# The opening of a decoder layer in the order of its loads: chunks of four token tiles in one PSUM bank, norms of four tiles together

## The chip, the cores and the metric

The kernel runs on one core of one Trainium2 chip. TensorE (PE) multiplies matrices into PSUM, ScalarE (ACT) and VectorE (DVE) do elementwise work, GpSimd (POOL) a little of the rest, and SyncE (SP) issues most DMAs. The metric is the time of one execution on the device in microseconds; the time shown for a kernel is the median of its runs. A separate, profiled execution leaves a trace, whose first and last instruction bound its span.

## The reference

A hybrid decoder layer for 1024 tokens of width 1024 (one sequence): a gated feed-forward half step, a mixing step (sliding-window attention beside a state-space model), and another feed-forward half step. Each has a norm ahead, with shift, scale and gate columns made from a conditioning vector. Only the beginning matters here:

```python
c_act = jax.nn.silu(c)
mod = c_act @ w_ada[l] + b_ada[l]
(sh1, sc1, ga1, sh2, sc2, ga2, sh3, sc3, ga3) = jnp.split(mod, N_MOD, axis=-1)

h = modulate(rms_norm(x, g_pre_ff1[l]), sh1, sc1)     # h * (1 + scale) + shift
f = swiglu(h, w1_gate[l], w1_up[l], w1_down[l])       # D_FF = 2816
x = x + 0.5 * ga1[:, None, :] * rms_norm(f, g_post_ff1[l])
```

All is float32.

## The kernel before, in words

**Layout.** The 1024 tokens are eight token tiles of 128 tokens by 1024 features (`xs`). The feed-forward needs features on partitions, so each tile is turned: eight blocks ("feature chunks" k = 0 to 7) of 128 x 128. The turned activations are eight arrays `hf[k]` (tags `q0` to `q7`) of 128 features by 1024 tokens. The gate and up weights are stored by units u of two blocks f; units 0 and 1 are computed directly, and units 2 to 21 by seven products of a fast 2x2 scheme each (order 1, 5, 6, 2, 7, 3, 4), with sums of quarters of the activations (`s12`, `s34`).

**Precision.** Every float32 operand is split in a high and a low part: ScalarE casts the high part (`act.copy` in `split`, L69) and VectorE subtracts (L70). `mm3` (L74 to L76) then issues three matmuls of 128x128 by 128x512 per pair.

**Norm and turning.** `norm_diag` (L1353 to L1358) squares a tile on ScalarE with an accumulated sum (L156), makes the reciprocal root with one ScalarE root and five tiny VectorE operations (L141 to L145, L151), and writes a 128x128 diagonal of it. Turning a tile is a product of its 128x128 blocks with that diagonal (L207), so that it is normed on the way; a product in float32 leaves two PE records. Four blocks of one tile go into one PSUM bank and are evicted one by one, 128x128 each, by ScalarE (L218, or L222, which modulates at once) or VectorE (L220).

**Modulation.** `ada_in(k)` makes shift and scale of chunk k: two weighted row sums of a 128x1024 block of `w_ada` (`ada_block`, L166) and one tiny operation (L190). `modulate` (L1367) applies them to 512 tokens of a chunk on VectorE, and `g1.block` splits the result. For r = 1 and the chunks 0 to 3 it is applied in the eviction (L222).

**Passes.** `g1.first(r, c)` multiplies half r of the tokens (512) and half c of the features (4 chunks) with units 0 and 1: 4 chunks x 2 units x 2 blocks x 3 = 48 matmuls, into banks `b0` to `b3` for r = 0 and `b4` to `b7` for r = 1. The order is (0,0), (1,0), (0,1), and in `second_half` (1,1), after which silu, product and the sums of `s12` and `s34` follow and the seven-product units begin.

**Order.** In the opening the program's order is a wish: a scheduler places each engine's instructions by a timeline of its own. `pinned` (L80) is the other way: the instructions that a function issues keep their written order on each engine. Before the change it is used from the seven-product units on, not in the opening. Loads go through SP's queue in the written order: the conditioning row, four token tiles, ada blocks of chunks 0 to 2, weights of units 0 and 1 (c = 0), ada of chunk 3, four token tiles, ada of 4 to 6, weights (c = 1), ada of 7.

Of the kernel before, what the change touches and what calls it, by code (L numbers as in the profile page):

```python
# [11 lines left out]
F32R = mybir.dt.float32r  # L12
I32 = mybir.dt.int32
AF = mybir.ActivationFunctionType
# [3 lines left out]
P = 128  # L18
D = 1024
# [11 lines left out]
def tile_layer(ctx: ExitStack, tc: tile.TileContext, a: dict, out: bass.AP, stage: str = "all"):  # L31
# [33 lines left out]
    def names(c, *idx):  # L65
        return tuple(f"{c}{i}" for i in idx)

    def split(hi, lo, src, eng=dve):
        act.copy(hi, src)  # L69
        eng.tensor_tensor(lo, src, hi.bitcast(F32), op=SUB)  # L70

    def mm3(psum, wh, wl, xh, xl, first, last, goes_on=False):

        pe.matmul(psum, wh, xh, start=first, stop=False, skip_group_check=goes_on)  # L74
        pe.matmul(psum, wh, xl, start=False, stop=False, skip_group_check=goes_on)  # L75
        pe.matmul(psum, wl, xh, start=False, stop=last, skip_group_check=goes_on)  # L76
# [3 lines left out]
    def pinned(f, *args, hold=True):  # L80


        traced = nc.cur_bb.bb.instructions
        n = len(traced)
        r = f(*args)
        for i in list(traced[n:]):
            prev = last_of.get(i.engine)
            if prev is not None:
                tc.add_manual_dep(
                    i, prev.name, mybir.DependencyInfo(mybir.DependencyClass.NoSync, mybir.DependencyReason.DATA),  # L90
                    reason="pinned",
                )
            if hold:
                last_of[i.engine] = i
        return r
# [52 lines left out]
    def rstd_of(ss, n, count):  # L148

        v = small(n, "rsv")  # L150
        dve.tensor_scalar(v, ss, 1.0 / count, EPS, op0=MUL, op1=ADD)  # L151
        return rsqrt(v, n)

    def row_rstd(src, junk):
        ss = small(1, "ss")
        act.activation(junk, src, AF.Square, accum_out=ss)  # L156
        return rstd_of(ss, 1, D)
# [15 lines left out]
    def mod(v):  # L173
        return modc[:, 8 * v : 8 * v + 8]
# [35 lines left out]
    def to_hf(t, xs, hf, *ns, scale=None):  # L210

        for b, n in enumerate(ns):
            pt = turned(xs, b, scale)
            for kk in range(4):
                k = 4 * b + kk
                dst = hf[k][:, t * P : (t + 1) * P]
                if n is None and b == 0:
                    act.copy(dst, pt[:, kk, :])  # L218
                elif n is None:
                    dve.tensor_copy(dst, pt[:, kk, :])  # L220
                elif b == 0:
                    act.activation(  # L222
                        dst, pt[:, kk, :], AF.Identity, scale=gsc[:, n, k : k + 1], bias=mod(3 * n)[:, k : k + 1]
                    )
# [67 lines left out]
    class Weights:  # L292
# [66 lines left out]
    class GateUp:  # L359
# [34 lines left out]
                self.put("s4", k, self.q(0, 1, k))  # L394


        def first(self, r, c, between=None):
            for k in range(4):
                x = self.A[f"a{r + 1}{c + 1}"][k]
                for u in range(2):  # L400
                    for f in range(2):
                        if c == 0 and k == 0:
                            self.pb[r, u, f] = bank(f"b{4 * r + 2 * u + f}")
                        w = self.wt.ops[u, f, c][:, :, k * P : (k + 1) * P]
                        mm3(self.pb[r, u, f], w[:, 0], w[:, 1], x[:, 0], x[:, 1], c == 0 and k == 0, c == 1 and k == 3)
                if between:
                    between(k)

# [678 lines left out]
    def prep_phases():  # L1087
# [258 lines left out]
    ada_rot = Rot(*names("a", 8, 9, 10, 11, 12, 13, 14, 15, 20, 21, 22, 23, 12, 13, 14, 15))  # L1346
# [12 lines left out]

    def ada_in(k, ws):  # L1360
        for j, w in zip((8 + k, k), ws):
            ada_block(j, w)
        scale_cols(0, 1, slice(k, k + 1))

    def modulate(r, k):
        x = g1.q(r, k // 4, k % 4)
        dve.tensor_scalar(x, x, gsc[:, 0, k : k + 1], mod(0)[:, k : k + 1], op0=MUL, op1=ADD)  # L1367

    def loads(c):

        xs = [load_in_order(f"a{4 * c + t}", x_d[0][4 * c + t]) for t in range(4)]
        ada = []
        for k in range(4 * c, 4 * c + 4):
            if k % 4 == 3:
                for u in range(2):
                    w1.load(u, c)
            ada.append([load_in_order(ada_rot(), a["w_ada"][j]) for j in (8 + k, k)])
        return xs, ada

    xs, ada = loads(0)  # L1380
    for t in range(4):
        with tc.high_priority():
            to_hf(t, xs[t], hf, None, None, scale=norm_diag(t, 0))
    for k in range(4):
        ada_in(k, ada[k])
        modulate(0, k)
        g1.block(0, 0, k)
    w1.first(0)
    g1.first(0, 0)
    xs, ada = loads(1)  # L1390
    for t in range(4):
        to_hf(4 + t, xs[t], hf, 0, None, scale=norm_diag(t, 1))
    for k in range(4):
        g1.block(1, 0, k)
    g1.first(1, 0)
    for k in range(4, 8):
        ada_in(k, ada[k - 4])
        for r in range(2):
            modulate(r, k)
            g1.block(r, 1, k - 4)  # L1400
    w1.first(1)
    g1.first(0, 1)
    sp.dma_start(sink, a["sinks"].partition_broadcast(P))

    def second_half(g):
# [207 lines left out]
```

## Time and profile before

| what | before |
|---|---|
| median of 3 runs | 1717.06 us (1717.0 to 1725.35) |
| the profiled execution's own time | 1718.82 us |
| its span in the trace | 1717.0 us |
| mean granted clock of TensorE | 0.985 |
| PE busy | 1652.9 us (96%) |
| VectorE, ScalarE busy | 1264.6 us (74%), 804.3 us (47%) |
| DMA | 249.08 MB |

A row of a timeline gives start, length, engine, line, operation, output and inputs, shapes and count, and in brackets the idle time ahead and what ended it. A row of groups gives count, busy time, mean ns and idle time ahead. The granted clock is 1.00 at full and 0.50 at half speed of TensorE.

### The profile page before, as it was taken

To read this page: it belongs to the slowest core of one execution; us is meant where nothing else is said; L and a number is where in the kernel's file an instruction comes from. 1 tells how busy PE (TensorE), PEld (TensorE's weight loads), DVE (VectorE), ACT (ScalarE), POOL (GpSimd) and SP (SyncE) were. 2 spreads that over 40 slices of the span, in tenths; PEclk is the share of its full clock that TensorE was granted. 3 is DMA by queue.
4 is the path that set the end of the run, shared out by engine and by line. 5 is a ranking of instruction groups with operands and counts; after the bars stand their busy time and mean duration, and the time that the engine had idled before them with its cause. 6 is when DMAs were issued, how large, how long until landed. Compare 5 with 4: busy or idle time off the path is not lost.

```text
span 1717.0 us, 22221 instructions
## 1 busy us (share of the span) xinstructions
PE 1652.9 (96%) x7669; PEld 1355.8 (79%) x7669; DVE 1264.6 (74%) x2470; ACT 804.3 (47%) x1654; POOL 124.8 (7%) x147
## 2 busy tenths in 40 slices
PE   5999999999999999899979998999999999999998
PEld 4878888787788878688757876878888888888886
DVE  7989997788779878735589378768666566678586
ACT  5633333553344557736555257633333333344562
POOL 0011100001100000000015044000000000000001
PEclk9999999999999999999989998999999999999999
DMA  9176752234395734410333126243232223494324
GB/s 377 42 257 239 244 187 93 104 129 149 128 368 183 232 115 147 150 37 13 96 90 87 49 76 197 84 172 117 104 117 92 93 92 120 154 375 125 110 97 161
DMA packets 112065, 249.08 MB, mean 145 GB/s; under 512 B 12088, under 2 KB 27744, under 8 KB 111952
## 3 DMA queue, kind: packets, MB, share of 16 engines
q1 hardware_dynamic: 102224, 214.12, 36.2%
q0 software_dynamic: 9152, 32.49, 5.6%
q8 instruction: 60, 0.98, 0.2%
q10 hardware_dynamic: 576, 1.05, 0.2%
q14 instruction: 53, 0.43, 0.1%
HBM read 187.87 MB, written 59.75 MB: 144 GB/s over the span
## 4 chain that ended last, share of the span: by engine, by line
PE 51%; DVE 4%; DMA 2%; ACT 1%; issue 1%; POOL 1%; SPq 0%; DVEq 0%; ACTq 0%; POOLq 0%
PE b L76 15%; PE b L75 15%; PE b L74 15%; PE b L751 1%; PE b L839 1%; PE b L841 1%; PE b L840 1%; PE b L785 1%; DMA r<-in_w_gu 1%; PE b L930 0%; PE b L205 0%; DMA w<-in_w_out 0%; ACT a L69 0%; POOL a L913 0%; PE b L926 0%
## 5 line engine op out<-in xcount | busy, mean ns | idle before, releaser
L74 PE MATMUL b<-a,w 128*128 128x512 f32 x1260 | 489.3, 393 | 15.1 <-ACT h L470 9.0
L75 PE MATMUL b<-a,w 128*128 128x512 f32 x1260 | 494.6, 392 | 5.6 <-DVE a L70 5.6
L76 PE MATMUL b<-a,w 128*128 128x512 f32 x1260 | 494.5, 392 | 1.4 <-DVE w L70 1.3
L74 PEld LDWEIGHTS b<-a,w 128*128 128x128 f32 x1260 | 238.0, 189 | 68.6 <-ACT h L470 11.5
L75 PEld LDWEIGHTS b<-a,w 128*128 128x128 f32 x1260 | 238.5, 189 | 56.3 <-DVE a L70 7.0
L76 PEld LDWEIGHTS b<-a,w 128*128 128x128 f32 x1260 | 238.6, 189 | 53.6 <-DVE w L70 3.8
L70 DVE TENSOR_TENSOR w<-r,w 128x512 fp32r<-128x512 f32 (+1 forms) x206 | 142.9, 694 | 137.9 <-ACT w L69 137.6
L75 PE MATMUL b<-w,r 128*128 128x512 f32 x528 | 205.5, 389 | 1.1 <-DVE w L70 1.1
L76 PE MATMUL b<-w,r 128*128 128x512 f32 x528 | 205.4, 389 | 0.0
L74 PE MATMUL b<-w,r 128*128 128x512 f32 x528 | 180.7, 389 | 0.0
L69 ACT CAST w<-r 128x512 fp32r<-128x512 f32 (+1 forms) x210 | 130.2, 623 | 94.3 <-DVE r L334 82.4
L69 ACT CAST r<-a 128x512 fp32r<-128x512 f32 x110 | 68.5, 623 | 149.5 <-PE b L76 107.8
L70 DVE TENSOR_TENSOR r<-a,r 128x512 fp32r<-128x512 f32 x110 | 75.7, 688 | 61.7 <-ACT r L69 61.6
L75 PEld LDWEIGHTS b<-w,r 128*128 128x128 f32 x528 | 99.1, 188 | 22.2 <-DVE w L70 1.6
L74 PEld LDWEIGHTS b<-w,r 128*128 128x128 f32 x528 | 99.1, 188 | 20.6
L76 PEld LDWEIGHTS b<-w,r 128*128 128x128 f32 x528 | 99.1, 188 | 20.5
L69 ACT CAST w<-t 128x512 fp32r<-128x512 f32 (+1 forms) x114 | 69.9, 613 | 83.7 <-DVE t L337 30.4
L70 DVE TENSOR_TENSOR w<-t,w 128x512 fp32r<-128x512 f32 (+1 forms) x114 | 79.7, 699 | 31.5 <-ACT w L69 31.3
L466 DVE TENSOR_TENSOR h<-h,b 128x512 f32<-128x512 f32 x120 | 82.2, 685 | 21.3 <-PE b L76 19.2
L454 ACT ACTIVATE h<-h 128x512 f32<-128x512 f32 x60 | 38.0, 633 | 117.8 <-DVE h L466 117.8
L70 DVE TENSOR_TENSOR w<-a,w 128x512 fp32r<-128x512 f32 x110 | 75.3, 685 | 0.2 <-ACT w L69 0.2
L74 PE MATMUL b<-a,a 128*128 128x512 f32 x182 | 72.2, 399 | 0.1
(376 smaller groups left out, 2554.4 us busy)
## 6 DMA issues: line engine op xcount, KB each, us to landing
r<-in_w_gu SPq DMA_DIRECT2D x88, 512.0 KB, 3.9
g_d<-h SPq DMA_DIRECT2D x154, 256.0 KB, 2.1
a<-g_d SPq DMA_DIRECT2D x110, 256.0 KB, 3.4
q<-in_w_ada POOLq DMA_DIRECT2D x48, 512.0 KB, 4.7
a<-in_w_d SPq DMA_DIRECT2D x88, 256.0 KB, 5.4
a<-in_w_ada SPq DMA_DIRECT2D x16, 512.0 KB, 10.2
a<-in_x SPq DMA_DIRECT2D x12, 512.0 KB, 6.8
x_d<-a SPq DMA_DIRECT2D x12, 512.0 KB, 3.7
```

Of the source, the lines that this page charges most:

```text
L69: act.copy(hi, src)
L70: eng.tensor_tensor(lo, src, hi.bitcast(F32), op=SUB)
L74: pe.matmul(psum, wh, xh, start=first, stop=False, skip_group_check=goes_on)
L75: pe.matmul(psum, wh, xl, start=False, stop=False, skip_group_check=goes_on)
L76: pe.matmul(psum, wl, xh, start=False, stop=last, skip_group_check=goes_on)
L454: act.activation(dst, src, AF.Silu)
L466: dve.tensor_tensor(dst, dst, pb, op=ADD)
L751: pe.matmul(pb[kv][:, m % 2, ks], qT[m][rows, t * P : (t + 1) * P], kT[rows, (t + 1 - nk) * P : (t + 1) * P], start=True, stop=True,)
L785: pe.transpose(pt[:, m, :], pr[4 * kv + m][:, b * P : (b + 1) * P], ident)
L839: pe.matmul(pb, hh, wh, start=k == 0, stop=False)
L840: pe.matmul(pb, hh, wl, start=False, stop=False)
L841: pe.matmul(pb, hl, wh, start=False, stop=k == NK - 1)
```

## The change

The opening becomes one function, `opening`, that is called through `pinned`, so that every engine keeps the order in which it is written.

- Token tiles 0 to 3 are squared one after another, and one root and one set of tiny operations makes the norms of all four (`squares`, `diagonals`); the same for tiles 4 to 7.
- `turn_in(c, k, ...)` turns chunk k of four tiles into one PSUM bank (128 x 512), instead of four chunks of one tile.
- `modulated` is a ScalarE activation with scale and shift columns over 128x512. For chunks 0 to 3 it reads PSUM; chunks 4 to 7 are copied out by ScalarE first and modulated later in place. VectorE evicts and modulates nothing in the opening any more.
- `first_part` is one chunk of `first`, for some of the units. For r = 0, c = 0 the turning of chunk 4 + k and its copy follow the matmuls of chunk k. For r = 1, c = 0 the pass is made for unit 0 first and unit 1 afterwards.
- 60 transposes of the identity matrix into a bank stand at the head of PE's order.
- The loads come in another order: four token tiles, ada of chunk 0, weights of units 0 and 1 (c = 0), ada of 1 to 3, four token tiles, ada of 4 and 5; ada of 6 and 7 and the weights of c = 1 are issued after the first four tiles have been turned.

```diff
+        def first_part(self, r, c, k, us):
+            x = self.A[f"a{r + 1}{c + 1}"][k]
+            for u in us:
+                for f in range(2):
+                    if c == 0 and k == 0:
+                        self.pb[r, u, f] = bank(f"b{4 * r + 2 * u + f}")
+                    w = self.wt.ops[u, f, c][:, :, k * P : (k + 1) * P]
+                    mm3(self.pb[r, u, f], w[:, 0], w[:, 1], x[:, 0], x[:, 1], c == 0 and k == 0, c == 1 and k == 3)
...
-    def norm_diag(t, c):
-
-        r = row_rstd(xs[t], slot(f"a{24 + t}", [D]))
-        diag = slot(f"h{4 * c + t}", [P])
-        dve.tensor_scalar(diag, ident, r[:, 0:1], None, op0=MUL)
-        return diag
...
-    def modulate(r, k):
-        x = g1.q(r, k // 4, k % 4)
-        dve.tensor_scalar(x, x, gsc[:, 0, k : k + 1], mod(0)[:, k : k + 1], op0=MUL, op1=ADD)
...
+    def modulated(r, k, src):
+
+        act.activation(g1.q(r, k // 4, k % 4), src, AF.Identity, scale=gsc[:, 0, k : k + 1], bias=mod(0)[:, k : k + 1])
+
+    def squares(c, ts):
+        for t in ts:
+            act.activation(slot(f"a{24 + t}", [D]), xs[4 * c + t], AF.Square, accum_out=ss[c][:, t : t + 1])
+
+    def diagonals(c):
+
+        r = rstd_of(ss[c], 4, D)
+        out = [slot(f"h{4 * c + t}", [P]) for t in range(4)]
+        for t in range(4):
+            dve.tensor_scalar(out[t], ident, r[:, t : t + 1], None, op0=MUL)
+        return out
+
+    def turn_in(c, k, diags, b):
+
+        pt = bank(f"b{b}", [4, P])
+        for t in range(4):
+            pe.matmul(pt[:, t, :], xs[4 * c + t][:, k * P : (k + 1) * P], diags[t], start=True, stop=True)
+        return pt.rearrange("p t q -> p (t q)")
+
+    def first_op(c, u, f):
+
+        op = slot(w1.w_rot() if c == 0 else w1.first_tags[2 * u + f], [2, 512], F32R)
+        split(op[:, 0], op[:, 1], w1.raw[u, c][:, f])
+        w1.ops[u, f, c] = op
+
+    def opening():
+
+        warm = bank("b0", [4, P])
+        for i in range(60):
+            pe.transpose(warm[:, i % 4, :], ident, ident)
+        squares(0, range(4))
+        diags = diagonals(0)
+        pts = [turn_in(0, k, diags, 4 + k) for k in range(4)]
+        for k in range(4):
+            if k == 0:
+                ada_in(0)
+                first_op(0, 0, 0)
+                first_op(0, 0, 1)
+            else:
+                ada_in(k)
+            modulated(0, k, pts[k])
+            g1.block(0, 0, k)
+            if k == 0:
+                first_op(0, 1, 0)
+                first_op(0, 1, 1)
+            g1.first_part(0, 0, k, (0, 1))
+            pt = turn_in(0, 4 + k, diags, 4 + k)
+            act.copy(g1.q(0, 1, k), pt)
+            if k >= 2:
+                squares(1, range(2 * k - 4, 2 * k - 2))
+        ada.extend([load_in_order(ada_rot(), a["w_ada"][j]) for j in (8 + k, k)] for k in range(6, 8))
+        for u in range(2):
+            w1.load(u, 1)
+        diags = diagonals(1)
+        pts = [turn_in(1, k, diags, 4 + k) for k in range(4)]
+        for k in range(4):
+            modulated(1, k, pts[k])
+            g1.block(1, 0, k)
+            if k % 2:
+                ada_in(4 + k // 2)
+        for k in range(4):
+            g1.first_part(1, 0, k, (0,))
+            if k % 2:
+                for i in (k - 1, k):
+                    pt = turn_in(1, 4 + i, diags, 6 + i % 2)
+                    act.copy(g1.q(1, 1, i), pt)
+        for k in range(4):
+            g1.first_part(1, 0, k, (1,))
+        for k in range(4, 8):
+            if k >= 6:
+                ada_in(k)
+            for r in range(2):
+                x = g1.q(r, 1, k - 4)
+                modulated(r, k, x)
+                g1.block(r, 1, k - 4)
+            if k == 4:
+                for u in range(2):
+                    for f in range(2):
+                        first_op(1, u, f)
+            g1.first_part(0, 1, k - 4, (0, 1))
+
+    xs = [load_in_order(f"a{t}", x_d[0][t]) for t in range(4)]
+    ada = [[load_in_order(ada_rot(), a["w_ada"][j]) for j in (8, 0)]]
+    for u in range(2):
+        w1.load(u, 0)
+    ada += [[load_in_order(ada_rot(), a["w_ada"][j]) for j in (8 + k, k)] for k in range(1, 4)]
+    xs += [load_in_order(f"a{t}", x_d[0][t]) for t in range(4, 8)]
+    ss = [small(4, "ss_in") for _ in range(2)]
+    ada += [[load_in_order(ada_rot(), a["w_ada"][j]) for j in (8 + k, k)] for k in range(4, 6)]
+    pinned(opening)
     sp.dma_start(sink, a["sinks"].partition_broadcast(P))
```

More of the change, by code (lines that the diff above doesn't have):

```diff
@@ L394, in s34 @@
                 self.put("s4", k, self.q(0, 1, k))
+        def first_part(self, r, c, k, us):
[6 more added lines that the diff above has]
+                    mm3(self.pb[r, u, f], w[:, 0], w[:, 1], x[:, 0], x[:, 1], c == 0 and k == 0, c == 1 and k == 3)
         def first(self, r, c, between=None):
             for k in range(4):
[L399 to L405, printed above, removed]
+                self.first_part(r, c, k, (0, 1))
                 if between:
@@ L1345, in tile_layer @@
         "s4": names("a", 8, 9, 10, 11), "a22": names("a", 12, 13, 14, 15)}, dve)
-    ada_rot = Rot(*names("a", 8, 9, 10, 11, 12, 13, 14, 15, 20, 21, 22, 23, 12, 13, 14, 15))
+    ada_rot = Rot(*names("a", 8, 9, 10, 11, 12, 13, 14, 15, 20, 21, 22, 23, 0, 1, 2, 3))
     def load_in_order(tag, src, shape=(D,)):
@@ L1351, in load_in_order, with ada_in @@
         return w
-    def norm_diag(t, c):
-        r = row_rstd(xs[t], slot(f"a{24 + t}", [D]))
-        diag = slot(f"h{4 * c + t}", [P])
-        dve.tensor_scalar(diag, ident, r[:, 0:1], None, op0=MUL)
-        return diag
-    def ada_in(k, ws):
-        for j, w in zip((8 + k, k), ws):
+    def ada_in(k):
+        for j, w in zip((8 + k, k), ada[k]):
             ada_block(j, w)
         scale_cols(0, 1, slice(k, k + 1))
-    def modulate(r, k):
-        x = g1.q(r, k // 4, k % 4)
-        dve.tensor_scalar(x, x, gsc[:, 0, k : k + 1], mod(0)[:, k : k + 1], op0=MUL, op1=ADD)
@@ L1369, in loads @@
[L1369 to L1374, printed above, removed]
-                for u in range(2):
[L1376 to L1402, printed above, removed]
+    def modulated(r, k, src):
+        act.activation(g1.q(r, k // 4, k % 4), src, AF.Identity, scale=gsc[:, 0, k : k + 1], bias=mod(0)[:, k : k + 1])
```

## The prediction

> **What bounds the kernel now.** The head of the page first, then the stages of the opening as stretches of the timeline (columns: length, then busy time and count on PE, PEld, DVE, ACT, POOL, then granted clock, DMA share, GB/s).
>
> ```profile
> span 1717.0 us, 22221 instructions
> ...
> PE 1652.9 (96%) x7669; PEld 1355.8 (79%) x7669; DVE 1264.6 (74%) x2470; ACT 804.3 (47%) x1654; POOL 124.8 (7%) x147
> ```
>
> ```profile
> 0.00:11.14 11.14, 0.00 (x1) 0.00 (x1) 1.14 (x7) 6.21 (x9) 0.74 (x7) 1.00 0.74 286
> 11.14:25.51 14.37, 10.95 (x64) 10.22 (x64) 13.24 (x48) 7.89 (x29) 0.00 (x0) 1.00 1.03 411
> 25.51:45.78 20.27, 15.73 (x72) 12.88 (x72) 20.27 (x65) 9.66 (x22) 0.00 (x0) 0.83 0.91 359
> 45.78:61.12 15.34, 15.34 (x90) 13.42 (x89) 14.03 (x35) 11.94 (x26) 0.00 (x0) 1.00 0.11 35
> 61.12:72.00 10.88, 10.88 (x49) 9.01 (x48) 10.88 (x19) 4.85 (x8) 0.00 (x0) 1.00 0.22 73
> 72.00:82.88 10.88, 10.88 (x49) 9.01 (x48) 10.88 (x19) 6.51 (x12) 0.00 (x0) 1.00 0.06 24
> 82.88:91.23 8.35, 5.83 (x26) 4.50 (x25) 8.28 (x14) 3.22 (x8) 3.38 (x6) 1.00 0.51 156
> ```
>
> TensorE is 96% busy, so a microsecond that it loses at the start is lost at the end. Each of the stretches from 25.51 to 82.88 holds 48 of the long matmuls (12 per chunk, 4 chunks, one pass); the rest of the counts are the short turning products. VectorE is full nearly everywhere, and DMA is nearly full to 45.78. After 91.23 PE hardly waits, so I measure the change by when the 217th long matmul starts, now 91.23: the third product after the opening. Three timeline rows of PE give the turning's price and the two costly gaps:
>
> ```profile
> 30.54 0.79 PE L75 MATMUL b<-a,w 128*128 128x512 f32 x1 [3.83 <-DVE a L70]
> ```
>
> ```profile
> 42.24 1.95 PE L207 MATMUL b<-h,a 128*128 128x128 f32 x16
> ```
>
> ```profile
> 91.23 0.50 PE L74 MATMUL b<-a,w 128*128 128x512 f32 x1 [2.52 <-ACT h L470]
> ```
>
> The two stretches of 10.88 are nothing but 48 long matmuls, so their pitch is 10.88/48 = 0.227. Two turned chunks (16 records) take 1.95: I count 0.9 for one that is followed by PE's own work, and 1.05 where somebody waits for its end. The clock, by stretches of 3.41 us:
>
> ```profile
> 20.37:23.78 3.41, 2.16 (x18) 1.86 (x16) 3.41 (x11) 1.68 (x7) 0.00 (x0) 1.00 1.02 406
> 23.78:27.19 3.41, 1.46 (x7) 0.75 (x5) 3.41 (x12) 2.20 (x5) 0.00 (x0) 1.00 1.03 410
> 27.19:30.61 3.42, 0.07 (x1) 0.07 (x1) 3.42 (x7) 3.04 (x6) 0.00 (x0) 0.50 1.03 410
> 30.61:34.02 3.41, 3.41 (x8) 2.73 (x9) 3.41 (x13) 2.49 (x8) 0.00 (x0) 0.50 1.02 408
> ...
> 88.63:92.05 3.42, 0.90 (x5) 0.69 (x5) 2.86 (x5) 1.46 (x3) 1.75 (x4) 1.00 0.64 186
> 92.05:95.46 3.41, 3.41 (x10) 2.65 (x9) 1.67 (x3) 0.76 (x2) 0.00 (x0) 0.50 0.98 357
> ```
>
> After a stretch that is 63% busy the clock stays; after 43% and 26% it is halved, and comes back only behind a full stretch. Eight matmuls fill 3.41 there, a pitch of 0.427: each such restart costs 8 x (0.427-0.227) = 1.6.
>
> **The prices.** ScalarE, then VectorE, groups by shape in the first 91 us (count, busy, mean ns):
>
> ```profile
> L69 ACT CAST a<-q 128x512 fp32r<-128x512 f32 x32 | 18.8, 625 | 16.9 <-DVE q L1367 9.0 <-DVE q L386 4.8 <-DVE q L382 2.2
> L156 ACT ACTIVATE a<-a 128x1024 f32<-128x1024 f32 x8 | 8.3, 1043 | 0.9 <-DMA a<-in_x 0.9
> L222 ACT ACTIVATE q<-b,modc,gsc 128x128 f32<-128x128 f32 x16 | 6.0, 457 | 4.0 <-PE b L207 4.0
> ...
> L218 ACT COPY q<-b 128x128 f32<-128x128 f32 x16 | 3.1, 276 | 6.4 <-PE b L207 6.4
> ...
> L141 ACT ACT_TABLE_LOAD x1 | 1.3, 1283 | 0.0
> ...
> L470 ACT COPY h<-b 128x512 f32<-128x512 f32 x1 | 0.6, 586 | 5.1 <-issue 5.1
> ```
>
> ```profile
> L70 DVE TENSOR_TENSOR a<-q,a 128x512 fp32r<-128x512 f32 x32 | 20.9, 686 | 0.0
> L166 DVE CUSTOM_DVE_ANT_0 a<-a,c,cols 128x1024 f32<-128x1024 f32 x16 | 20.4, 1277 | 0.0
> L220 DVE COPY q<-b 128x128 f32<-128x128 f32 x32 | 7.0, 281 | 1.3 <-PE b L207 1.3
> L1367 DVE TENSOR_SCALAR q<-q,gsc,modc 128x512 f32<-128x512 f32 x12 | 6.2, 541 | 0.0
> ...
> L143 DVE SCALAR_TENSOR_TENSOR s<-s 128x1 f32<-128x1 f32 x8 | 1.1, 153 | 0.1
> ```
>
> The new modulation out of PSUM (128x512, scale and bias as columns) stands in no row. From below it is the plain copy, 0.59; from above four of L222, 1.83. I take L222 plus the size step that separates L218 from L470: 0.457 + (0.586-0.276) = 0.77, nearest in kind. An ada step is two of L166 and a scale column: 2 x 1.28 + 0.2 = 2.8.
>
> **What it removes.** From VectorE 32 evictions (7.0), 12 modulations (6.2) and 30 of 40 tiny norm operations (30 x 0.153 = 4.6): 17.8 us. ScalarE loses 32 small evictions (9.1) and six roots and gains 16 x 0.77 + 8 x 0.59 = 17. All of this would help if these engines stayed fed; the order decides that.
>
> **The start.** The first token tile lands when its square begins, and three more of 0.52 MB follow at 411 GB/s, 1.28 each: 7.2 + 3.8 = 11.1.
>
> ```profile
> 7.24 1.06 ACT L156 ACTIVATE a<-a 128x1024 f32<-128x1024 f32 x1 [0.87 <-DMA a<-in_x]
> ```
>
> Its square and accumulator read 1.2, table load 1.3, root and four tiny operations 1.0, four diagonals of 128x128 (L220's size) 0.85: 15.4. Ada step to 18.2, modulation 19.0, cast 19.6, subtraction (L70) 20.3: the first chunk of matmuls starts there, where now it starts at 25.51 and, for good, at 30.54. The 60 warming transposes have this record, one for each transpose (64 for 8 tiles of 8 chunks):
>
> ```profile
> L205 PE MATMUL b<-ident,q x64: 270/272/421, 661.6 to 729.7; 128*128 128x128 f32 x64
> ```
>
> At half clock a record of this size is 0.9/8 x 2 = 0.22, so 60 take at most 13.5 from the identity's making, done before 15.4: nothing on the path. But if the clock rises after the first stretches, they end near 9, PE idles six microseconds, and the clock has fallen again by 15.4. Then the four turned chunks take 7.2 instead of 3.6 and end at 22.6: 0 to 2.3 more.
>
> **The loop of the first four chunks.** Every engine's queue keeps the written order here. ScalarE's is: modulate chunk k, cast it, then copy out turned chunk 4+k, then modulate chunk k+1. That copy waits for PE, where the turning stands behind the twelve matmuls of chunk k. So the next modulation, cast and subtraction, with VectorE behind them, wait for the end of PE's work, and PE then waits for them. One turn is 12 x 0.227 + 1.05 + copy 0.59 + modulation 0.77 + cast 0.62 + subtraction 0.69 + three hand-overs of 0.04 = 6.6, with PE idle 2.8 of it. VectorE's ada step (2.8) and the DMA are hidden inside. Chunks start at 20.3, 26.9, 33.5 and, since two squares (2 x 1.04) stand ahead of the fourth modulation, 42.2; the pass ends at 44.9, as now (45.78), in spite of the early start. Its last turning and copy end at 46.6; only then come two squares (2.3), the batched norm (1.2) and diagonals (0.85): the second four tiles turn at 51.0. PE idles 5.0.
>
> **The rest of the opening.** Four turnings, 24 matmuls and four turnings take 12.6, to 63.6; two copies free the banks, and the other 24 end at 69.9, 8.8 later than now (61.12). The third pass is limited by chunks 6 and 7. ScalarE makes four modulations, four casts and four weight casts from 64.9 on (4 x 1.3 + 4 x 0.53 = 7.3, 72.2), the last subtraction ends at 72.9, and behind it in VectorE's order stand ada 6 (2.8), modulation, cast, subtraction (2.1): matmuls of chunk 6 at 77.9, where PE had been done at 75.4; chunk 7 likewise at 84.2 after 3.6 idle. The pass ends at 86.9 (now 72.0) and the fourth at 97.8 (now 82.88): +14.9.
>
> The moved loads cost nothing: ada 6 and 7 and two weight tiles leave SP after the last turning at 46.0, and a weight load takes this long:
>
> ```profile
> r<-in_w_gu SPq DMA_DIRECT2D x88, 512.0 KB, 3.9
> ```
>
> Six in a row land by 46.0 + 3.9 + 5 x 1.28 = 56.3, their first user runs at 64.9. Without those 9 us the third pass would wait one for one. Behind them in SP's queue stand the sinks and the weights of units 2 and 3, used after 98.
>
> After the fourth pass two products (24 matmuls, 5.4) cover 97.8 to 103.2. The eviction for which PE now waits (L470, 0.59 long) began 91.23 - 0.63 - 82.88 = 7.7 after the pass, behind VectorE's queue; with that queue shorter, two silus (at most 0.59 each), a multiplication and four sums (0.69 each) alone are 4.6. So the third product starts at 103.2 to 106.1, against 91.23; if PE no longer idles there it saves the 1.6 of the restart. At full clock that is **+10.4 to +14.9, taken as +12.**
>
> **The clock.** PE now idles 2.8, 2.8, 4.9, 5.0, 2.5 and 3.6. Stretches of 43% and 26% were punished, one of 63% was not; 2.8 idle leaves between 18% (in one stretch) and 59% (split over two). I count five of six restarts at 1.6: 8, between 3.2 (the two long ones alone) and 6 x 1.6 + 2.3 = 12. Sum **+20**: 1718.8 of the profiled run becomes 1739. The median of the runs shown stands 1.8 below that run (1717.06), so **1737**; own range 1731 (+14) to 1744 (+27).
>
> The page "TensorE: Matmul & The Clock Gate" of the Trainium skill, section "HAM oscillation", puts the rule as no idle gaps above about 3.4 us. The 2.52 gap at 91.23, halved afterwards, speaks against it here.
>
> **Rivals.** (a) Only gaps above one stretch of 3.41 count: three restarts, 4.8, so +16.8 and 1734. Against it stands the row of 88.63. 0.14. (It is what the rule of the Trainium skill's page "TensorE: Matmul & The Clock Gate", section "HAM oscillation", would give.) (b) The clock never falls, +12: 1729; the warming speaks for it, the same row against it. 0.08. (c) A restart regularly costs two stretches, since a segment of 3.6 rarely fills one: 6 x 3.2 + 12 = +31, 1748. 0.08. (d) Not slower: the eviction of chunk 4+k runs behind modulation k+1, because the executed order is not the written one. That is decided at ScalarE's copy alone; then a turn costs PE's own 3.6, chunks run 20.3 to 34.7, the second tiles turn at 37, the third pass ends near 66 and the fourth at 76.8, 6 early: 1711. For it: chunk k+1's inputs are there in time. Against it: the pinned order names every instruction. 0.10. (e) VectorE, full in all rows to 91, was the only limit, and its 17.8 us come through until PE is solid from 20.3 on: 216 x 0.227 + 12 chunks x 0.9 = 59.8, third product at 80.1, and no restart: -12.7, 1704. It needs everything of (d) and no gap at all. 0.08. The forecast itself: 0.52.
>
> **Chances and range.** About 0.5% (8.6 us: 1708.5 to 1725.6) is what a measurement of this kernel can tell from no change. Slower: the forecast, (a), (c) and most of (b), 0.79. Within: (d) and a little of (b), 0.13. Faster: (e), 0.08. The range leaves out (d) and (e), 0.18, and reaches over (c): 1722 to 1748.
>
> **What would show it.** In the changed profile: first long matmul near 20.3 to 22.6; then twelve-matmul bursts 6 to 9 apart with PE waiting for the subtraction and ScalarE waiting for PE before each 128x512 copy; a gap of about 5 before the second tiles turn, near 51 to 57; gaps ahead of chunks 6 and 7 behind the ada steps; half-clock stretches in between; the third product at 103 to 115. Bursts 3.6 apart would show (d), and the forecast wrong; a third product before 95 would too.

## The result, and the profile after

The changed kernel takes **1739.6 us** (median of 4 runs, 1736.48 to 1743.38). The kernel before, run beside it, takes 1720.26 (4 runs, 1717.0 to 1725.35). The ratio is 1.011, with a 95% interval of 1.0087 to 1.0133: the change makes the kernel slower by about 19 us. The prediction was 1737.0.

The profiled execution of the changed kernel took 1743.38 us. The head of its page:

```profile
span 1741.6 us, 22246 instructions
...
PE 1670.7 (96%) x7729; PEld 1371.0 (79%) x7729; DVE 1254.1 (72%) x2396; ACT 811.5 (47%) x1640; POOL 120.0 (7%) x147
```

VectorE has 74 instructions less, as intended, and 10.5 us less to do (before: x2470 and 1264.6). The prediction had put 17.8, from the lengths of single records. Records that follow each other without a pause overlap (the ada block at 80.36 is 1.28 long, and the next operation starts 1.20 behind it), and busy time counts the overlap once. TensorE's share of the span is still 96%. The 60 more PE instructions are the warming transposes.

The opening in stretches of the timeline (length, then busy time and count on PE, PEld, DVE, ACT, POOL, then granted clock, DMA share, GB/s). Each stretch ends where PE's work changes: the first turned chunks, the first long matmul, the end of the first pass, the second turning, the second pass and so on, up to the 217th long matmul.

```profile
15.27:21.42 6.15, 6.15 (x32) 6.15 (x33) 5.79 (x13) 3.49 (x6) 0.00 (x0) 0.56 1.03 411
21.42:49.50 28.08, 19.49 (x83) 15.03 (x81) 9.85 (x19) 7.72 (x13) 0.00 (x0) 0.88 0.52 205
49.50:53.88 4.38, 0.01 (x2) 0.04 (x1) 1.23 (x7) 2.87 (x6) 0.00 (x0) 1.00 0.91 311
...
98.70:108.07 9.37, 6.15 (x29) 4.76 (x27) 9.37 (x17) 4.75 (x10) 3.37 (x6) 1.00 0.64 202
```

In the row from 21.42 to 49.50, the loop of the first four chunks, VectorE works 9.85 of 28.08 us and ScalarE 7.72. Before the change, VectorE worked all 20.27 us of the stretch that answers to this one. Both engines are now mostly idle, and PE is idle for 8.6 us as well. No engine is the bound here; they wait for each other in a ring. The third product starts at 108.07, where it started at 91.23 before: **+16.8**.

The timeline of PE shows the ring (start, length, line, operation, shapes and count; in brackets the idle time ahead and what ended it). L1381 turns chunks, L74 and L75 are long matmuls.

```profile
1.36 9.51 PE L1394 MATMUL b<-ident 128*128 128x128 f32 x60 [1.36 <-POOL ident masks.py:199]
15.27 6.39 PE L1381 MATMUL b<-h,a 128*128 128x128 f32 x32 [4.40 <-DVE h L1374]
21.42 0.48 PE L74 MATMUL b<-a,w 128*128 128x512 f32 x1
...
24.28 1.05 PE L1381 MATMUL b<-h,a 128*128 128x128 f32 x8
27.34 0.68 PE L74 MATMUL b<-a,w 128*128 128x512 f32 x1 [2.01 <-ACT a L69]
...
35.06 0.50 PE L74 MATMUL b<-a,w 128*128 128x512 f32 x1 [2.00 <-ACT a L69]
35.79 0.51 PE L75 MATMUL b<-a,w 128*128 128x512 f32 x1 [0.23 <-DVE a L70]
...
43.53 0.49 PE L74 MATMUL b<-a,w 128*128 128x512 f32 x1 [4.08 <-ACT a L69]
...
53.88 5.44 PE L1381 MATMUL b<-h,a 128*128 128x128 f32 x32 [4.37 <-issue]
...
85.99 0.50 PE L75 MATMUL b<-a,a 128*128 128x512 f32 x1 [0.55 <-DVE a L70]
92.99 0.51 PE L74 MATMUL b<-a,a 128*128 128x512 f32 x1 [1.49 <-ACT a L69]
...
108.07 0.50 PE L74 MATMUL b<-a,w 128*128 128x512 f32 x1 [3.22 <-ACT h L473]
```

The bursts begin at 21.42, 27.34, 35.06 and 43.53, so they are 5.9, 7.7 and 8.5 apart. PE waits ahead of the last three for ScalarE's cast (L69). On ScalarE's side, the turns that lead to the bursts at 27.34 and 35.06:

```profile
25.37 0.58 ACT L1412 COPY q<-b 128x512 f32<-128x512 f32 x1 [4.51 <-PE b L1381]
25.85 0.78 ACT L1363 ACTIVATE q<-b,modc,gsc 128x512 f32<-128x512 f32 x1
26.66 0.62 ACT L69 CAST a<-q 128x512 fp32r<-128x512 f32 x1
...
33.09 0.59 ACT L1412 COPY q<-b 128x512 f32<-128x512 f32 x1 [5.81 <-PE b L1381]
```

ScalarE is idle for 4.51 and 5.81 us ahead of these two copies, and what ends that idle time is PE's turning. Only then come the modulation and the cast that PE needs for its next burst. The first turn in full: PE's turning ended at 24.28 + 1.05 = 25.33, the copy starts at 25.37, the cast ends at 27.28, the burst starts at 27.34.

Last, the clock in stretches of 3.41 us (columns as above):

```profile
24.09:27.50 3.41, 1.40 (x11) 1.18 (x9) 0.32 (x4) 1.88 (x3) 0.00 (x0) 1.00 1.03 413
27.50:30.91 3.41, 3.36 (x8) 2.31 (x9) 2.99 (x6) 0.00 (x0) 0.00 (x0) 0.50 1.02 407
30.91:34.33 3.42, 2.15 (x14) 1.74 (x12) 0.00 (x0) 1.24 (x2) 0.00 (x0) 1.00 1.04 402
34.33:37.74 3.41, 2.45 (x10) 1.82 (x11) 2.70 (x4) 0.65 (x2) 0.00 (x0) 1.00 0.38 150
...
41.15:44.57 3.42, 0.81 (x2) 0.48 (x3) 0.69 (x1) 2.29 (x4) 0.00 (x0) 1.00 0.00 0
44.57:47.98 3.41, 3.41 (x9) 2.67 (x8) 0.00 (x0) 0.00 (x0) 0.00 (x0) 0.50 0.00 0
...
51.39:54.81 3.42, 0.94 (x8) 0.97 (x9) 1.71 (x9) 1.02 (x3) 0.00 (x0) 1.00 1.01 355
54.81:58.22 3.41, 3.41 (x18) 3.41 (x18) 0.69 (x1) 2.76 (x4) 0.00 (x0) 0.50 1.00 394
```

Behind a stretch that PE filled to 1.40 of 3.41 (41%), to 0.81 (24%) and to 0.94 (28%) the clock is halved. Behind 2.15 (63%) it stays. The gap of 2.00 ahead of 35.06 is as long as the one ahead of 27.34, but it is spread over two stretches of 63% and 72%, and costs no restart.

### The profile page after: what moved, and what is told of

The parts are those of the page before. It is cut to its first block, busy times and chain, and to the rows that moved or that the text cites. A ratio compares the mean times of both kernels' runs of the same rounds, so it can differ in the third digit from the quotient of the medians.

```text
span 1741.6 us, 22246 instructions
## 1 busy us (share of the span) xinstructions
PE 1670.7 (96%) x7729; PEld 1371.0 (79%) x7729; DVE 1254.1 (72%) x2396; ACT 811.5 (47%) x1640; POOL 120.0 (7%) x147
## 3 DMA queue, kind: packets, MB, share of 16 engines
q10 hardware_dynamic: 576, 1.05, 0.2%
## 4 chain that ended last, share of the span: by engine, by line
PE 80%; DVE 9%; ACT 4%; DMA 3%; issue 2%; SPq 0%; POOL 0%; DVEq 0%; ACTq 0%; POOLq 0%
PE b L76 24%; PE b L75 24%; PE b L74 24%; DVE a L70 1%; PE b L1381 1%; PE b L754 1%; PE b L842 1%; PE b L844 1%; PE b L843 1%; PE b L788 1%; DMA h<-in_w_ada 1%; ACT a L69 1%; DVE w L70 1%; DMA r<-in_w_gu 1%; DVE h L432 1%
## 5 line engine op out<-in xcount | busy, mean ns | idle before, releaser
L74 PE MATMUL b<-a,w 128*128 128x512 f32 x1260 | 496.1, 396 | 25.0 <-ACT h L473 11.2
L75 PE MATMUL b<-a,w 128*128 128x512 f32 x1260 | 495.4, 393 | 2.3 <-DVE a L70 2.2
L74 PEld LDWEIGHTS b<-a,w 128*128 128x128 f32 x1260 | 239.7, 190 | 79.3 <-ACT h L473 13.6
L75 PEld LDWEIGHTS b<-a,w 128*128 128x128 f32 x1260 | 239.8, 190 | 53.4 <-DVE a L70 4.1
L75 PE MATMUL b<-w,r 128*128 128x512 f32 x528 | 205.5, 389 | 1.4 <-DVE w L70 1.4
L74 PE MATMUL b<-w,r 128*128 128x512 f32 x528 | 180.7, 389 | 0.0
L69 ACT CAST w<-r 128x512 fp32r<-128x512 f32 (+1 forms) x210 | 130.3, 622 | 98.8 <-DVE r L334 83.6
L69 ACT CAST r<-a 128x512 fp32r<-128x512 f32 x110 | 68.5, 623 | 148.5 <-PE b L76 111.6
L75 PEld LDWEIGHTS b<-w,r 128*128 128x128 f32 x528 | 99.1, 188 | 22.4 <-DVE w L70 1.8
L74 PEld LDWEIGHTS b<-w,r 128*128 128x128 f32 x528 | 99.1, 188 | 20.5
L69 ACT CAST w<-t 128x512 fp32r<-128x512 f32 (+1 forms) x114 | 69.9, 613 | 84.0 <-DVE t L337 30.5
L74 PE MATMUL b<-a,a 128*128 128x512 f32 x182 | 70.2, 395 | 3.7 <-DVE r L961 2.2
```

## The experiments

Theory 1 is the prediction's: in ScalarE's written order, the copy of a turned chunk stands ahead of the next modulation and waits for PE, which closes the ring. The rivals are that the cost comes from the restarts of the clock, from the warming, from VectorE's remaining queue (the ada steps), or is scatter between executions. In the timelines below, a line number is that of the kernel shown. The kernel before was run again beside each set: its median was 1719.42 for the first four, 1718.79 for the next three and 1718.48 for the last two, and the ratios are against these.

### The copy behind the next chunk's modulation

```diff
-            pt = turn_in(0, 4 + k, diags, 4 + k)
-            act.copy(g1.q(0, 1, k), pt)
+            late = g1.q(0, 1, k), turn_in(0, 4 + k, diags, 4 + k)
```

In the next turn of the loop, `act.copy(*late)` stands right behind `g1.block(0, 0, k)`, that is, behind modulation and cast; the last copy stands behind the loop.

> The changed kernel with one thing altered: in the loop over the first four chunks ScalarE's copy of turned chunk 4+k stands behind the modulation and cast of chunk k+1 instead of ahead of them. Theory 1 (that copy, waiting for PE in ScalarE's queue, sets the pace): the first four chunks' matmuls start about 5.0 apart (ada step 2.8, modulation 0.78, cast 0.62, subtraction 0.69) instead of 6.4 to 8.5, the second four tiles turn near 40 to 42 instead of 53.9, the third product starts near 95 to 98 instead of 108.1, and the time is 1722 to 1729, some 10 to 16 below the changed kernel. Theory 2 (the order of the loads or VectorE's ada steps set the pace, the copy is only seen waiting): the second tiles turn within 3 us of 53.9 and the time stays within 5 us of 1739.6.

Measured: **1721.49** us (11 runs), ratio 1.0019 (1.0004 to 1.0034). PE's timeline of this kernel:

```profile
25.04 0.50 PE L74 MATMUL b<-a,w 128*128 128x512 f32 x1 [0.27 <-ACT a L69]
...
29.71 0.50 PE L74 MATMUL b<-a,w 128*128 128x512 f32 x1 [0.22 <-ACT a L69]
...
40.74 5.44 PE L1381 MATMUL b<-h,a 128*128 128x128 f32 x32 [1.95 <-issue]
...
95.57 0.79 PE L74 MATMUL b<-a,w 128*128 128x512 f32 x1 [2.24 <-ACT h L473]
```

The first two bursts shown are 4.67 apart, the third follows at the same distance, the waits ahead of them 0.2 to 0.3, and the second tiles turn at 40.74 rather than 53.88, 13.1 earlier. The third product starts 12.5 earlier. Moving four copies gives back 1739.6 - 1721.5 = 18 us of the 19, to half a microsecond below the expected 1722 to 1729: theory 1 holds. What remains in the medians is within what can be told from no change. In the traces, 12.5 of the 18 arise up to the third product, which still starts 4.3 later than before the change (95.57 against 91.23).

The pace of 4.67 is still not PE's own. ScalarE's modulations for the second and third burst wait 3.46 and 2.76 us for the scale column of VectorE's ada step, and VectorE's subtractions wait 1.5 us for ScalarE's cast: a smaller ring is left between these two engines.

### PE kept busy by adding zeros

```diff
             act.copy(g1.q(0, 1, k), pt)
+            for i in range((8, 8, 17, 18)[k]):
+                pe.matmul(g1.pb[0, 0, 0], zero, g1.A["a11"][0][:, 0], start=False, stop=False)
```

`zero` is a 128x128 tile of zeros that ScalarE makes ahead of the root, so the result is unchanged. The ring stays; only PE's idle time in it is filled.

> The changed kernel with extra work on PE: after the turning in each of the four rounds of the loop, 8, 8, 17 and 18 long matmuls with a weight tile of zeros into an open bank (they add nothing), which fill PE's idle time in the loop. The order and all waits of the other engines stay. Theory 1 (idle gaps cost twice, since the clock is halved after them): although PE does 51 matmuls more, no half-clock stretch is left between 27 and 54, the two bursts that now take 3.6 to 4.7 shrink to 2.7, the third product starts 3 to 5 earlier than 108.1, and the time is 1734 to 1737. Theory 2 (the clock is no part of the loss in the loop, or the added matmuls stand in the way): the third product starts at 108 or later and the time is 1739 to 1745.

Measured: **1732.44** us (5 runs), ratio 1.0072 (1.0056 to 1.0089). The timeline of PE, then the granted clock over the whole loop:

```profile
24.16 2.07 PE L1417 MATMUL b<-a,zero 128*128 128x512 f32 x8
...
45.57 4.34 PE L1417 MATMUL b<-a,zero 128*128 128x512 f32 x18
50.19 3.81 PE L1381 MATMUL b<-h,a 128*128 128x128 f32 x32 [0.28 <-PE b L1417]
...
102.75 0.50 PE L74 MATMUL b<-a,w 128*128 128x512 f32 x1 [3.25 <-ACT h L473]
```

```profile
19.19:50.19 31.00, 29.48 (x146) 23.15 (x144) 12.65 (x28) 11.85 (x22) 0.00 (x0) 1.00 0.64 245
```

With 51 matmuls more the kernel is 7.2 us faster: the clock is full from 19.19 to 50.19, and the second turning takes 3.81 instead of 5.44. The third product starts 5.3 earlier. Of these, 0.9 were there ahead of the first added matmul (the first burst starts at 20.49 instead of 21.42); the other 4.4 arise from there to the end of the second turning, and are what the restarts of the loop cost in the trace, within the three to five microseconds put down for them. The medians move by more, to below the expected 1734 to 1737; the rest is not placed. By the medians, the loss splits in two: the ring without these restarts costs 1732.4 - 1719.4 = 13.0, the restarts up to 7.2.

### No warming transposes

```diff
-        warm = bank("b0", [4, P])
-        for i in range(60):
-            pe.transpose(warm[:, i % 4, :], ident, ident)
```

> The changed kernel without the 60 transposes of the identity at the head of PE's order. Theory 1 (they end near 11 and the clock has fallen again when the tiles are turned at 15.3, so they do nothing): the four turned chunks still take about 6.4, the third product stays within 1.5 us of 108.1, the time within 3 us of the changed kernel. Theory 2 (the warming pays): the start is later by 2 us or more and so is the end.

Measured: **1740.18** us (4 runs), ratio 1.0123 (1.0104 to 1.0141), as with the warming (1739.6). The third product's row:

```profile
108.21 0.50 PE L74 MATMUL b<-a,w 128*128 128x512 f32 x1 [3.22 <-ACT h L473]
```

The 60 transposes neither cost nor bring anything. They end at 10.87, PE then waits 4.40 for the diagonals, and the four turned chunks run at half clock all the same (6.39 us for 32 records, 6.38 without the warming, where the zeros' second turning took 3.81 at full clock).

### The order left to the scheduler

```diff
-    pinned(opening)
+    opening()
```

> The changed kernel with the opening called without its pinned order, so that the scheduler places the instructions by its own timeline; operations, tiles and loads are the same. Theory 1 (the written order is what costs, not the new operations): the long waits of ScalarE for the copies vanish or move, the second four tiles turn before 50, and the time is 1718 to 1732. Theory 2 (the new operations and the new order of the loads cost the time in any order): 1735 or more.

Measured: **1710.66** us (12 runs), ratio 0.9957 (0.9942 to 0.9972). This is better than expected, and below the kernel before. ScalarE's timeline shows the order that the scheduler chose:

```profile
20.22 0.78 ACT L1363 ACTIVATE q<-b,modc,gsc 128x512 f32<-128x512 f32 x1 [3.51 <-PE b L1381]
21.03 0.62 ACT L69 CAST a<-q 128x512 fp32r<-128x512 f32 x1
21.55 0.77 ACT L1363 ACTIVATE q<-b,modc,gsc 128x512 f32<-128x512 f32 x1
22.24 0.59 ACT L1412 COPY q<-b 128x512 f32<-128x512 f32 x1
22.72 0.62 ACT L69 CAST a<-q 128x512 fp32r<-128x512 f32 x1
24.06 0.59 ACT L1412 COPY q<-b 128x512 f32<-128x512 f32 x1 [0.72 <-PE b L1381]
```

The modulation of the second chunk (21.55) stands ahead of the first copy (22.24). ScalarE waits 0.72 for PE where it waited 4.51 and 5.81. So the change's own operations, in another order, make the kernel faster by 0.43%, just under the 0.5% that was set as the smallest difference to tell, with an interval that lies below 1. The loss was in the written order, not in what is computed where.

### The scheduler's order with 100 transposes

```diff
-        for i in range(60):
+        for i in range(100):
```

This and the line of the section above.

> The same version without the pinned order, with 100 warming transposes instead of 60. Theory 1 (the warming fails only because it ends 4 us too early): PE is busy to 13.5 or later, the first four turned chunks take 3.6 to 4.5 instead of about 6, and the time is 1 to 3 below 1710.7. Theory 2 (PE's start is not on the path there, since VectorE's first ada step and the first subtraction end at about 20 in any case): the chunks are turned faster, but the time stays within 1.5 of 1710.7.

Measured: **1709.98** us (7 runs), ratio 0.9949 (0.993 to 0.9968). First the start of PE's work with the scheduler's order and 60 transposes, then with 100:

```profile
15.45 6.76 PE L1381 MATMUL b<-h,a 128*128 128x128 f32 x40 [5.29 <-DVE h L1374]
```

```profile
15.41 3.84 PE L1381 MATMUL b<-h,a 128*128 128x128 f32 x32 [1.50 <-DVE h L1374]
```

Warmed until 1.5 us ahead of its use, PE turns four chunks in 3.84 at full clock. The time stays within a microsecond of the 1710.66: PE's start is not what sets the end. This is the fastest version of the study, 0.51% below the kernel before, though it can't be told from the one with 60.

### Modulation on VectorE, in the scheduler's order

```diff
-        act.activation(g1.q(r, k // 4, k % 4), src, AF.Identity, scale=gsc[:, 0, k : k + 1], bias=mod(0)[:, k : k + 1])
+        dve.tensor_scalar(g1.q(r, k // 4, k % 4), src, gsc[:, 0, k : k + 1], mod(0)[:, k : k + 1], op0=MUL, op1=ADD)
```

The opening is left to the scheduler here too.

> The changed opening without the pinned order (as in the run with the scheduler, 1710.7), but with the 16 modulations of 128x512 on VectorE instead of ScalarE, 16 x 0.6 = 10 us back on VectorE. Theory 1 (the scheduler's version beats the kernel before because VectorE, which was full to 91, has less to do): the third product starts 4 to 9 later than its 85.8 and the time is 1715 to 1720. Theory 2 (it is faster because of the chunked turning, the batched norms or the order of the loads, and VectorE is not the limit): within 3 us of 1710.7.

Measured: **1713.66** us (12 runs), ratio 0.9967 (0.9955 to 0.9979). VectorE is busy 71.92 of the 75 us from 15 to 90, against 63.92 with the modulation on ScalarE and 73.66 in the kernel before. The third product starts at 88.52, 2.7 later than the 85.8 of the scheduler's version, where theory 1 had 4 to 9. The time is 3.0 higher, at the edge of the second expectation, and the intervals of the two kernels overlap. In this order VectorE's relief is worth about 3 us, if it can be told at all; where the rest of the scheduler's gain over the kernel before comes from isn't settled.

### An order written by hand for all engines

On top of the first experiment: 100 transposes, the first weights of the second unit ahead of the first modulation and their low parts on GpSimd, the two halves of an ada step on both sides of a chunk's subtraction, and ada 6 and 7 earlier. The core of the diff:

```diff
-        split(op[:, 0], op[:, 1], w1.raw[u, c][:, f])
+        split(op[:, 0], op[:, 1], w1.raw[u, c][:, f], pool if (c, u) == (0, 1) else dve)
...
+            if 0 < k < 3:
+                ada_block(9 + k, ada[k + 1][0])
...
+            if k < 3:
+                ada_block(k + 1, ada[k + 1][1])
+                scale_cols(0, 1, slice(k + 1, k + 2))
```

> A pinned order in which no engine waits for work that could come later: the copy of chunk 4+k behind the modulation of chunk k+1 as in the run with the later copy; on VectorE the first half of ada step k+1 ahead of the subtraction of chunk k, the first ada block ahead of the norms, ada steps 6 and 7 right behind step 5; the low parts of the weights of unit 1 (c = 0) on GpSimd; 100 warming transposes instead of 60. Theory (waits put into the order are the loss, operations and loads are sound): the first four chunks start some 3.6 to 4 apart, the first chunk near 18.5 to 20, the second four tiles turn at 35 to 37 (40.7 with the later copy alone), the third product starts at 84 to 90, and the time is 1704 to 1714. Rival (VectorE's total work, or the landing of the second four tiles near 29, is the limit behind it): second tiles turn after 39 and the time is 1717 or more.

Measured: **1716.01** us (12 runs), ratio 0.9985 (0.9972 to 0.9999), a miss: the second tiles turn at 39.91 rather than 35 to 37, and the third product starts at 90.11, just behind the expected 84 to 90. ScalarE's row ahead of the second norm's root, and a row each of VectorE and GpSimd:

```profile
38.00 0.58 ACT L1422 COPY q<-b 128x512 f32<-128x512 f32 x1 [1.97 <-PE b L1381]
38.48 0.21 ACT L141 ACTIVATE s<-s 128x4 f32<-128x4 f32 x1
```

```profile
19.23 1.24 DVE L70 TENSOR_TENSOR a<-q,a 128x512 fp32r<-128x512 f32 x1 [1.71 <-ACT a L69]
```

```profile
17.44 2.49 POOL L70 TENSOR_TENSOR w<-r,w 128x512 fp32r<-128x512 f32 x2 [16.13 <-ACT w L69]
```

The last copy waits 1.97 for PE, and the root (L141), on which the diagonals and the second turning depend, stands behind it: the same fault as in the change, at another place. The first experiment has it there too, with a wait of 1.93. The subtraction took 1.24 instead of 0.69 while GpSimd worked on the weights.

### Ada 6 and 7 earlier

The first experiment, and the two last ada steps moved from the third pass to the place right behind the second tiles' modulations:

```diff
+        for k in (6, 7):
+            ada_in(k)
...
-            if k >= 6:
-                ada_in(k)
```

> The version with the later copy (1721.5), with one thing more: ada steps 6 and 7 stand right behind step 5 in VectorE's order instead of ahead of the modulations of chunks 6 and 7. Theory 1 (PE's gaps of 0.55, 1.47 and 0.41 in the third and fourth pass wait for these steps): the gaps vanish, the restart behind them too, the time falls by 2 to 5 to 1716 to 1720. Theory 2 (VectorE's whole queue sets the third product, whatever its order): the gaps ahead of the third product grow by what is saved, and the time stays within 1.5 of 1721.5.

Measured: **1714.38** us (8 runs), ratio 0.9973 (0.9961 to 0.9985), 7 below the first experiment and faster than before by 0.27%, which is less than what was set as the smallest difference to tell. PE's row:

```profile
90.53 0.50 PE L74 MATMUL b<-a,w 128*128 128x512 f32 x1 [3.79 <-ACT h L473]
```

The gaps of 0.55, 1.47 and 0.41 ahead of chunks 6 and 7 are gone. The one ahead of the third product grew from 2.24 to 3.79, as the rival had it, but the third product is 5.0 earlier: the ada steps ahead of chunks 6 and 7 did cost time, somewhat more than expected.

### The changed kernel again

No edit; a second profile.

> The changed kernel itself, unaltered, for a second profile and more runs beside the other versions: in the first profile 16.8 us of its delay were there when the third product started, and 7.7 more came between 898 and 1122, in the mixing stage, which the change doesn't touch. Theory 1 (those 7.7 are scatter of one execution, in half-clock stretches): the third product starts again at 107 to 109.5, the delay in the mixing stage is a different one, below 5, and the median is 1735 to 1740. Theory 2 (the later start shifts something in the mixing stage each time): again 6 or more are lost there.

Measured: **1739.16** us (4 runs), ratio 1.0111 (1.0094 to 1.0128); the profiled execution took 1734.78. This was to settle a part of the loss that lies outside the opening. In the first profile the delay against the kernel before was 16.8 at the third product and 24.6 at the end (spans of 1741.6 and 1717.0), so 7.8 arose behind the opening, most of them in the mixing stage. That stage in the kernel before, in the changed kernel, and in the changed kernel again:

```profile
883.00:1102.00 219.00, 203.24 (x1058) 164.75 (x1059) 157.88 (x291) 115.45 (x220) 66.70 (x43) 0.94 0.31 99
```

```profile
900.00:1125.00 225.00, 206.98 (x1058) 168.00 (x1055) 158.58 (x289) 113.92 (x219) 62.07 (x43) 0.92 0.30 96
```

```profile
897.00:1118.00 221.00, 203.84 (x1067) 165.40 (x1064) 160.69 (x292) 114.86 (x220) 63.57 (x43) 0.94 0.30 98
```

The same work took 219, 225 and 221 us, at a clock of 0.94, 0.92 and 0.94. In the second profile the delay is 14.8 at the third product (105.99, a microsecond below the expectation) and 16.0 at the end (span 1733.0): only 1.2 arose behind the opening. The version without the warming, which has the same ring, lies between, with 17.0 and 21.2 (span 1738.2). And the first experiment, 4.3 late at the third product, ends 0.2 ahead of the kernel before (span 1716.8). So the part behind the opening scatters by several microseconds in single executions, and the change's place is the opening. But the medians differ by 19 to 21 and the traces, at the third product, by 15 to 17; whether the 4 or so between are scatter too, or follow from the later start, isn't shown.

The second profile shows one thing more: the clock after the loop's short gaps.

```profile
22.04:25.45 3.41, 2.19 (x14) 1.79 (x12) 2.03 (x5) 1.18 (x2) 0.00 (x0) 1.00 1.02 405
25.45:28.87 3.42, 2.41 (x9) 1.79 (x10) 2.65 (x4) 0.70 (x2) 0.00 (x0) 1.00 1.02 407
28.87:32.28 3.41, 1.78 (x12) 1.43 (x11) 0.53 (x3) 1.56 (x3) 0.00 (x0) 1.00 1.03 411
```

The gaps ahead of the second and third burst are 2.00 long here too, but the stretches of 3.41 us begin at other points of the work: the first gap (24.23 to 26.24) is split at 25.45, and the stretches are filled to 64%, 71% and 52%. Neither gap is followed by half clock, and the bursts start at 20.33, 26.24 and 32.65, so 5.9 and 6.4 apart instead of 5.9 and 7.7. Whether a gap of 2 us costs a restart differs between two executions of one kernel.

## Why the prediction was right

The forecast was 1737, with its own range of 1731 to 1744 (1722 to 1748 with the rivals that it reaches over); the time is 1739.6. The mechanism came as predicted; that the number is so near is in part luck, as the last step shows. By its steps:

- **The ring in the loop** was right. ScalarE's copy waits for PE, the next modulation, cast and subtraction wait behind it, and the first experiment shows that this order carries most of the loss: 18 of the 19 us in the medians, 12.5 of the 16.8 at the third product. The turns were put at 6.6, 6.6 and, with two squares, 8.7, longer with restarts; they took 5.9, 7.7 and 8.5.
- **The start** was right: 20.3 at full clock, up to 22.6 at half; it is 21.42, with the turning at half clock behind the idle time that the warming leaves.
- **The price of the modulation** was right. This row groups it over the first 108 us:

```profile
L1363 ACT ACTIVATE q<-b,modc,gsc 128x512 f32<-128x512 f32 x8 | 6.2, 777 | 5.0 <-PE b L1381 3.0 <-DVE gsc L190 2.1
```

- **PE's idle time per turn** was put at 2.8 and is 2.0 to 2.2: PE's first matmul (L74) needs the cast only, and the subtraction is awaited by the second (L75, 0.23 more), while another matmul runs. The two long gaps came as predicted (4.08 and 4.37 against 4.9 and 5.0).
- **The gaps ahead of chunks 6 and 7** are the step that failed in size: 2.5 and 3.6 predicted; 0.55 and 1.49 + 0.40 measured. The third and fourth pass were taken as one behind the other. But the fourth pass stands outside the pinned order, and the scheduler put its matmuls of the chunks that were ready into that wait (48 of the two passes' 96 start ahead of 84.98, chunks 6 and 7 of both follow), so much less of it was lost.
- **The third product's gap** was put at 0 to 2.9 (103.2 to 106.1, behind two products that end at 103.2), and at the lower end its restart was counted as saved. It is 3.22, and the restart stayed. VectorE was expected to have a shorter queue there; it works 9.37 of the 9.37 us from 98.70 to 108.07: the sums of this product (L432) stand there between the sums and subtractions of other chains. The eviction now comes 107.43 - 98.70 = 8.7 behind the pass, where it came 7.7 behind it before.
- **The clock** was put at five restarts of six gaps, 8 us, and that was too many. In the first profile three of those six gaps were punished, the two long ones and the first of the loop; in the second profile the two long ones alone. Those at the start and at the third product stayed besides. A gap of 2.00 that is spread over two stretches cost nothing, and chunks 6 and 7 had no long gap. Three restarts at 1.6 are 4.8; the experiment with zeros gives 4.4 in the trace and up to 7.2 in the medians. At full clock the prediction had +12 (10.4 to 14.9); that experiment shows +11.5 at the third product and +13.0 in the medians.
- **The sum** of +20 was worked out for the third product, and there the two profiles have +16.8 and +14.8: the restarts and the gaps of the third pass were put too high, the third product's gap too low. The medians differ by 19.3 all the same; the 4 or so between are not placed, and no step of the prediction stands for them. The base moved too: 1717.06 when the forecast was made, 1720.26 beside the changed kernel. So the near hit owes something to luck.

Of the rivals, (d) was the one that decides at ScalarE's copy. It did not happen in the changed kernel. The first experiment makes just that exchange, and doesn't bear out (d)'s price: turns of 4.67 instead of 3.6, the second tiles at 40.74 instead of 37, 1721.5 instead of 1711, since VectorE's ada steps and ScalarE still wait for each other. The scheduler's order, which is free to move everything else too, has (d)'s numbers: 1710.7, the second tiles at 37.91, and turns of 3.6 (PE's turned chunks of the version with 100 transposes start at 23.60, 27.24 and 30.87). Rival (e), VectorE as the only limit, falls: emptied, it brought nothing as long as the order stood. Rival (a), that only gaps above one stretch count, falls at the row of 24.09, where a gap of 2.01 halved the clock; that its three restarts and its +16.8 stand in the first profile is chance, since one of the three follows that short gap. Rival (b), that the clock never falls, goes by the same row. Rival (c), two stretches for each restart, doesn't fit the first profile, where each of the three in the loop has one stretch of half clock (27.50, 44.57, 54.81). The Trainium skill, page "TensorE: Matmul & The Clock Gate", section "HAM oscillation — how this bites in real kernels", names gaps above about 3.4 us as those that throttle; by that, the burst at 27.34 would have kept its clock, and the trace does not agree.

## What to carry to other kernels

On an engine that runs its queue in order, a copy that waits for another engine must not stand ahead of what that engine needs next; look for a long idle time that ends with the engine you wanted to feed, in front of a short instruction. Relieving a busy engine brings nothing while such a ring sets the pace, and the idle time then shows on all engines at once. A written order must be costed per queue, or the scheduler's order tried beside it.

## What the runs showed of the hardware

- **Gaps of 2 us can halve the clock**, by where they fall. In the changed kernel, stretches of 3.41 us that PE filled to 41%, 28% and 24% were followed by half clock, while 63% and 72% kept it. Between them it went either way: stretches of 45% and 50% (from 47.98 and 37.74 of the same profile) kept the clock, one of 43% (from 23.78 in the kernel before) and one of 45% (from 78.40 in the first experiment) lost it.
- **Idle time of PE can be worth filling.** 51 matmuls with zeros saved 7.2 us in the medians and 4.4 in the opening's trace.
- **Warming that ends early does nothing.** 60 transposes that end 4.4 us ahead of the first use left it at half clock; 100 that end 1.5 us ahead, in the scheduler's order, gave 3.84 us for what had taken 6.39. The kernel's time didn't move by it (1709.98 against 1710.66).
- **A subtraction on VectorE took 1.24 us instead of 0.69** while GpSimd ran two of the same form. The Trainium skill, page "GPSIMD Engine Reference", section "1. Specifications", says that GpSimd shares its way to the on-chip memory with VectorE, with contention where VectorE reads two inputs from there; this row agrees, but no run was made to test it.
